# Sums of squares through TensorE: full-precision tiles against one pre-added tile in a high and a low rounded part

## The chip, the core and the metric

The kernel runs on one core of a Trainium2 chip. A core has a matrix engine (TensorE, in the profile PE, its weight loads PEld), a vector engine (VectorE, DVE), a scalar engine (ScalarE, ACT), a general engine (GpSimd, POOL) and a sync engine (SP) that here only issues DMAs. Each engine works through its own list of instructions in order and waits on semaphores for the others. The metric is device time in microseconds (us) from one execution; lower is better.

## The reference

One layer of a diffusion transformer over 512 latent tokens with a prefix of 256 context tokens, in float32, model width 2048. Cut to what matters here:

```python
def _rmsnorm(x, w):
    y = x * rsqrt(mean(x * x, axis=-1) + EPS)
    return y * w

h  = _modulate(_rmsnorm(x,  norm1_w), sh1,  s1)     # 512 latent tokens
hc = _modulate(_rmsnorm(xc, norm1_w), sh1c, s1c)    # 256 context tokens
p = h @ w_in                                        # also hc @ w_in
c_q  = _rmsnorm(p[..., 3072:3456], q_norm_w)        # rank 384, latent tokens only
c_kv = _rmsnorm(p[..., 3456:3712], kv_norm_w)       # rank 256, latent and context
...                                                 # 8 differential heads, 8 latent (MLA) heads
o_da = _rmsnorm(o_da, subln_w) * 0.8                # per head, over its 128 features
x = x + g1 * (concat(o_da, o_mla) @ w_o)
h2 = _modulate(_rmsnorm(x, norm2_w), sh2, s2)       # second norm, over 2048 features
x = x + g2 * _conv_ffn(h2, ...)                     # gated MLP, inner width 5632
return _rmsnorm(x, final_w)
```

Each norm needs, per token, a sum of squares over features.

## The kernel before

Activations lie with features on the 128 partitions and tokens along the free dimension, so a tile is 128 features by 512 latent tokens (`T`), or by 768 tokens (`TT`) with the context. A sum over features is a sum over partitions. The kernel gets it from TensorE: a 128x128 matrix of ones (`ones32`) as weights and a tile of squares as the moving operand give the sum, on every partition, in PSUM; several tiles are summed by accumulating their matmuls. `rstd` (L157) turns the sum into 1/sqrt by Ln and Exp on ScalarE and one Newton step in four VectorE instructions.

The large products split each float32 operand into a high part rounded to the type fp32r and a low part, the rest (`split`, L77: a ScalarE copy and a VectorE subtract), and run three fp32r matmuls, L104 to L106 (`mm3`). The sums of squares instead run their matmul on the float32 tiles themselves; the trace shows each as two MATMUL records. L numbers are lines of the kernel before.

The work runs in stages, by the time in the profiled execution:

- 0 to 180 us: modulation, first norm, the first five feature blocks.
- 180 to 350: `latent_norm` (L428) of the two `ckv` tiles, then ten blocks of input projection (`feature`, L457), each two weight blocks of 1024 columns loaded by `wblock` (L87), then `latent_norm` of the three `cq` tiles, where the value projection starts. Meanwhile VectorE runs the products of the modulation weights with the conditioning vector (`gemv`, L166, recorded at L171).
- 350 to 480: value projection, in two halves. 480 to 700: the eight differential heads.
- 700 to 890: the eight MLA heads. After the scores of head `h` the kernel calls `sub_norm(h)` (L646), which fetches a differential head's output, squares it (L651), sums it (L653), and scales it in place. Between, `weighted_values` (L517) transposes the probabilities (L522), splits them (`wth`, `wtl`, L80 and L81) and multiplies with the values (`po`). For every even head but the last, `latent_pair` (L591) makes the next two heads' queries, keys and values.
- 890 to 1060: output projection. For the first twelve output tiles `add_square` (L699) squares on ScalarE and adds into `ss` on GpSimd (L705). The last four tiles are done by `last_projection` (L998): each is gated on VectorE (L732), stored by a DMA issued from GpSimd (L1022) and squared (L1017), and the second norm's sum is accumulated in PSUM from `ss` (L1036) and the squares of the last four tiles (L1037, L1039, L1042, L1046).
- 1060 to 2440: the gated MLP and the final norm.

Up to about 1010 us a planner orders the instructions of each engine: it walks the program with its own estimates of durations and places what it believes to be ready, so that an edit can also move instructions around it. From the last quarter of the output projection on, the order is written out by hand (`manual_schedule`, for PE, ACT, DVE and SP), in the order of the code. Tiles of a tag share a ring of `bufs` buffers: the tag `nq` in `latent_norm` has one, so that each square waits for the matmul of the one before.

Of the kernel before, what the change touches and what calls it, by code (L numbers as in the profile page):

```python
# [17 lines left out]
P = 128  # L18
D = 2048
KT = D // P  # L20
T = 512
C = 256
TT = T + C
# [29 lines left out]
def layer_kernel(ctx: ExitStack, tc: tile.TileContext, small, rope, c_row, cc_row, x_t, ctx_t, ada, ada_k,  # L53
                 w_g0, w_f, w_v, w_uqn, w_uqr, w_ukv, w_o, w_up0, w_up, w_dn, out_t):
    nc = tc.nc
    pe, ve, sc, gp = nc.tensor, nc.vector, nc.scalar, nc.gpsimd

    cst = ctx.enter_context(tc.tile_pool(name="cst", bufs=1))
# [6 lines left out]
    def nm(s):  # L65
        n[0] += 1
        return f"{s}{n[0]}"
# [55 lines left out]

    ident = cst.tile([P, P], F32, name="ident")
    make_identity(nc, ident)
    ones32 = cst.tile([P, P], F32, name="ones32")
    ve.memset(ones32, 1.0)
    epst = cst.tile([P, 1], F32, name="epst")
    ve.memset(epst, EPS)
# [17 lines left out]
    def apply_rope(out, ps, tmp):  # L147
        t2 = tmp()
        ve.tensor_tensor(out, ps, ropet[:, 0, :], op=ALU.mult)
        ve.stream_shuffle(t2, ps, mask=[i ^ 16 for i in range(32)])  # L150
        ve.tensor_tensor(t2, t2, ropet[:, 1, :], op=ALU.mult)
        ve.tensor_tensor(out, out, t2, op=ALU.add)

    def exp_ln_tables():
        tc.keep_in_program_order(sc.preload_act_table_set("natural_log_exp_and_others"))
# [110 lines left out]
    with tc.manual_schedule(engines={mybir.EngineType.PE, mybir.EngineType.Activation, mybir.EngineType.DVE,  # L266
# [14 lines left out]
        for wide in (cb, ccb):  # L281
            sc.activation(wide[0:1], wide[0:1], AF.Silu)
            s_ = s_tile()
            for j in range(4):
                t = s_[:, j * 512:j * 512 + 512] if j < 2 else b_tile()
# [4 lines left out]
        for kt in range(KT):  # L290
            sq = st.tile([P, TT], F32, tag="h", name=nm("sq"), bufs=3) if kt else sqs
# [52 lines left out]
    for kt in range(KT):  # L344
# [8 lines left out]
        with tc.high_priority():  # L353
            h = st.tile([P, TT], F32, tag="h", name=nm("h"), bufs=3)
            for i, (x, c, m, (hh, hl)) in enumerate(((xs[kt], slice(0, T), modx, hx[kt]),
                                                     (ct, slice(T, TT), modc, hc[kt]))):
                b, t, r = m[:, kt:kt + 1], h[:, c], rinv[:, c]
# [5 lines left out]
        for f in range(5):  # L363
            w = (wh[:, f * P:(f + 1) * P], wl[:, f * P:(f + 1) * P])
# [62 lines left out]

    def latent_norm(tiles, width, dim, wname, dst):  # L428
        s = s_tile()
        cuts = [(0, T)] if width == T else [(0, T), (T, width)]  # L430
        for i, t in enumerate(tiles):
            q = kv.tile([P, TT], F32, tag="nq", name=nm("nq"), bufs=1)
            sc.square(q[:, :width], t)
            for c0, c1 in cuts:
                pe.matmul(s[:, c0:c1], ones32, q[:, c0:c1], start=i == 0, stop=i == len(tiles) - 1)
        r, t1 = (kv.tile([P, TT], F32, tag=g, name=nm(g), bufs=1) for g in ("nr", "n1"))
        t2 = kv.tile([P, TT], F32, tag="nq", name=nm("n2"), bufs=1)
        rstd(r[:, :width], s[:, :width], dim, t1[:, :width], t2[:, :width])
        for i, t in enumerate(tiles):
            ve.scalar_tensor_tensor(out=t, in0=t, scalar=col(wname, i), in1=r[:, :width], op0=ALU.mult, op1=ALU.mult)  # L440
            hl = [kvs.tile([P, TT], F32R, tag=g, name=nm(g))[:, :width] for g in ("kh", "kl")]
            split(hl[0], hl[1], t)
            put(dst[i], hl)
# [9 lines left out]
    q = rtmp()  # L453
# [176 lines left out]
    mb = None  # L630
# [14 lines left out]

    def sub_norm(h):  # L646

        q, rs, t2 = (mb.tile([P, T], F32, tag=g, name=nm(g), bufs=1) for g in ("sq", "sr", "s2"))
        oraw[h] = b2k()
        nc.sync.dma_start(oraw[h], o_d[h])  # L650
        sc.square(q, oraw[h])  # L651
        po = b_tile("f", 2)
        pe.matmul(po, ones32, q, start=True, stop=True)  # L653
        rstd(rs, po, P, mb.tile([P, T], F32, tag="sq", name=nm("s1"), bufs=1), t2)
        ve.scalar_tensor_tensor(out=oraw[h], in0=oraw[h], scalar=subs, in1=rs, op0=ALU.mult, op1=ALU.mult)

# [341 lines left out]
    def last_projection(i):  # L998
        kb, w = jobs[i][1], [h[0] for h in ready[i][:2]]
        if kb < 6:  # L1000
            for j in range(2):
                for d in range(4):
                    project(live["o"], d, kb * 2 + j, w)
            cast(i + 2)
            low(i + 2)
            return
        outs, xr = live["o"], live["xr"]

        def both(d, kbs=(6, 7)):
            for k in kbs:  # L1010
                for kt in (2 * k, 2 * k + 1):
                    project(outs, d, kt, [h[0] for h in ready[i - kb + k][:2]])

        def square(src, c=slice(0, T)):
            if c.start == 0:
                live["q"] = wo.tile([P, T], F32, tag="sq", name=nm("sq"), bufs=2)
            sc.square(live["q"][:, c], src[:, c])  # L1017
            return live["q"]

        def put(d):  # L1020
            gated(12 + d, outs[d], xr[d])
            gp.dma_start(x1_d[12 + d], x1[12 + d])  # L1022
            return square(x1[12 + d])

        if kb == 6:
            both(0)
            both(1)
            cast(i + 2)
            low(i + 2)
            live["q0"] = put(0)  # L1030
            return
        s = s_tile()
        po = s[:, :T]
        both(2)
        q1 = put(1)
        pe.matmul(po, ones32, ss, start=True, stop=False, skip_group_check=True)  # L1036
        pe.matmul(po, ones32, live["q0"], start=False, stop=False, skip_group_check=True)  # L1037
        both(3, (6,))
        pe.matmul(po, ones32, q1, start=False, stop=False, skip_group_check=True)  # L1039
        both(3, (7,))  # L1040
        q2 = put(2)
        pe.matmul(po, ones32, q2, start=False, stop=False, skip_group_check=True)  # L1042
        for c in halves:
            gated(15, outs[3], xr[3], c)
            q3 = square(x1[15], c)
            pe.matmul(po[:, c], ones32, q3[:, c], start=False, stop=True, skip_group_check=True)  # L1046
        gp.dma_start(x1_d[15], x1[15])
        wo.release()
        mem["ff"] = tc.alloc_tile_pool(name="ff", bufs=1, reuse_waits="tile")
        hp = mem["hp"] = tc.alloc_tile_pool(name="hp", bufs=1, side="right", reuse_waits="tile")  # L1050
        r = mem["r"] = hp.tile([P, T], F32, name="nr")
        n1, n2 = (hp.tile([P, T], F32, tag="h", name=nm("n"), bufs=6) for _ in range(2))
        for c in halves:
            sc.activation(r[:, c], po[:, c], AF.Ln, bias=epst, scale=1.0 / D)
            sc.activation(r[:, c], r[:, c], AF.Exp, scale=-0.5)
            ve.tensor_scalar(out=n1[:, c], in0=po[:, c], scalar1=1.0 / D, scalar2=EPS, op0=ALU.mult, op1=ALU.add)
        norm_tiles(0)
        norm_tiles(1)
        for c in halves:
            ve.scalar_tensor_tensor(out=n2[:, c], in0=r[:, c], scalar=-0.5, in1=r[:, c], op0=ALU.mult, op1=ALU.mult)  # L1060
            ve.tensor_tensor(n2[:, c], n2[:, c], n1[:, c], op=ALU.mult)
# [352 lines left out]
```

## Time and profile before

| what | value |
|---|---|
| three runs | 2440.68, 2437.37, 2435.56 us |
| median | 2437.37 us |
| profiled execution, its own time from first to last instruction | 2439.6 us |
| PE busy | 2367.0 us, 97% |
| DVE, ACT, POOL busy | 1735.5 (71%), 1117.0 (46%), 220.2 (9%) us |
| mean granted TensorE clock | 0.992 |

The page gives busy time by engine, the span in 40 slices, the queues, a chain of work that ended last, and groups of instructions. The trace behind it can be asked for windows (busy time of each engine in a stretch) and for a timeline (start, duration, engine, line, operation, output and inputs, and in square brackets the idle time before it and what ended that). Durations of successive matmuls overlap; their pace is the distance between starts.

### The profile page before, as it was taken

What the parts mean: (1) busy time and instruction counts of PE and PEld (TensorE: products, weight loads), DVE (VectorE), ACT (ScalarE), POOL (GpSimd) and SP (SyncE); (2) the same over time, 40 slices, a digit from 0 to 9 for tenths busy, and PEclk for the clock granted to TensorE, in tenths of its full rate; (3) what the DMA queues carried; (4) which work ended last, traced back from release to release, by engine and by line L of the source; (5) the groups of instructions that cost most, each with busy time, mean ns of one, the idle gap of its engine ahead of it and who ended that gap; (6) DMA issues with size and microseconds to landing.
All of it is one profiled execution on the core that took longest, in us unless ns stands there. A gap on an engine that the chain in (4) does not pass through costs nothing.

```text
span 2439.6 us, 32889 instructions
## 1 busy us (share of the span) xinstructions
PE 2367.0 (97%) x12758; PEld 1978.4 (81%) x12758; DVE 1735.5 (71%) x2316; ACT 1117.0 (46%) x1696; POOL 220.2 (9%) x244
## 2 busy tenths in 40 slices
PE   6999999999999999999999999999999999999998
PEld 3678877777777778889888888888888888888888
DVE  6668876388868878378667676767666666666667
ACT  4432121155646542245445454545454545454545
POOL 0000000121100003100111111111111111111110
PEclk9999999999999999999999999999999999999999
DMA  8758889555411149423555555555555565556573
GB/s 300 279 211 309 327 319 330 181 166 144 127 59 44 44 161 349 146 87 113 147 130 143 134 140 137 137 139 136 141 134 143 132 143 132 141 135 140 133 188 111
DMA packets 130707, 403.32 MB, mean 165 GB/s; under 512 B 14323, under 2 KB 25075, under 8 KB 122099
## 3 DMA queue, kind: packets, MB, share of 16 engines
q1 hardware_dynamic: 104118, 350.87, 43.7%
q0 software_dynamic: 25280, 49.30, 11.6%
q8 instruction: 100, 1.64, 0.3%
q10 hardware_dynamic: 1152, 1.05, 0.1%
q14 instruction: 57, 0.47, 0.1%
HBM read 331.68 MB, written 69.48 MB: 164 GB/s over the span
## 4 chain that ended last, share of the span: by engine, by line
PE 76%; DVE 8%; issue 7%; ACT 4%; DMA 3%; POOL 2%; SPq 0%; DVEq 0%; ACTq 0%; POOLq 0%
PE y L1133 11%; PE b L105 9%; PE b L104 9%; PE b L106 9%; PE z L1133 5%; PE y L1135 5%; PE s L104 3%; PE s L105 3%; PE s L106 3%; PE z L1135 3%; PE s L510 3%; PE x L1133 2%; DMA ada<-in_ada 2%; PE b L206 1%; PE f L104 1%
## 5 line engine op out<-in xcount | busy, mean ns | idle before, releaser
L989 DVE TENSOR_TENSOR wl<-wr,wh 128x1024 fp32r<-128x1024 f32 x144 | 176.4, 1225 | 157.8 <-ACT wh L981 157.1
L981 ACT CAST wh<-wr 128x1024 fp32r<-128x1024 f32 x144 | 151.0, 1049 | 234.0 <-PE b L105 118.5
L104 PE MATMUL b<-ah,wh 128*128 128x512 f32 (+1 forms) x664 | 256.8, 387 | 0.0
L105 PE MATMUL b<-al,wh 128*128 128x512 f32 (+1 forms) x664 | 256.7, 387 | 0.0
L106 PE MATMUL b<-ah,wl 128*128 128x512 f32 (+1 forms) x664 | 255.9, 385 | 0.0
L1154 POOL DMA_DIRECT2D x_d<-xs x160 | 139.6, 1004 | 1162.6 <-ACT xs L1153 1159.3
L989 DVE TENSOR_TENSOR wl<-rb,wh 128x1024 fp32r<-128x1024 f32 x123 | 150.0, 1220 | 126.9 <-ACT wh L981 126.8
L981 ACT CAST wh<-rb 128x1024 fp32r<-128x1024 f32 x123 | 129.2, 1050 | 185.7 <-PE b L105 116.1
L989 DVE TENSOR_TENSOR wl<-ws,wh 128x1024 fp32r<-128x1024 f32 x123 | 150.1, 1220 | 90.1 <-ACT wh L981 90.1
L80 ACT CAST wh<-wr 128x1024 fp32r<-128x1024 f32 (+3 forms) x102 | 99.2, 972 | 217.0 <-PE b L106 62.1
L171 DVE CUSTOM_DVE_ANT_0 ada<-ada,cb,smt 128x2048 f32<-128x2048 f32 x64 | 152.5, 2382 | 54.6 <-DMA ada<-in_ada 54.2
L981 ACT CAST wh<-ws 128x1024 fp32r<-128x1024 f32 x123 | 128.2, 1043 | 130.3 <-DVE ws L943 44.3
L1133 PE MATMUL y<-a2k,wh 128*128 128x512 f32 x656 | 164.0, 392 | 0.0
L81 DVE TENSOR_TENSOR wl<-wr,wh 128x1024 fp32r<-128x1024 f32 (+3 forms) x102 | 116.9, 1146 | 62.1 <-ACT wh L80 61.7
L104 PE MATMUL b<-a2k,wh 128*128 128x512 f32 (+1 forms) x376 | 141.6, 377 | 5.9 <-ACT a2k L838 4.3
L106 PEld LDWEIGHTS b<-ah,wl 128*128 128x128 f32 x664 | 124.8, 188 | 25.7
L104 PEld LDWEIGHTS b<-ah,wh 128*128 128x128 f32 x664 | 125.1, 188 | 22.9
L105 PEld LDWEIGHTS b<-al,wh 128*128 128x128 f32 x664 | 125.1, 188 | 21.9
L105 PE MATMUL b<-a2k,wh 128*128 128x512 f32 (+1 forms) x376 | 140.8, 374 | 0.0
L106 PE MATMUL b<-a2k,wl 128*128 128x512 f32 (+1 forms) x376 | 140.0, 372 | 0.0
L1133 PEld LDWEIGHTS y<-a2k,wh 128*128 128x128 f32 x656 | 118.6, 189 | 21.6
L1133 PE MATMUL y<-b2k,wh 128*128 128x512 f32 x410 | 107.8, 393 | 0.0
(454 smaller groups left out, 5757.2 us busy)
## 6 DMA issues: line engine op xcount, KB each, us to landing
ada<-in_ada SPq DMA_DIRECT2D x64, 1024.0 KB, 6.4
rb<-in_w_up SPq DMA_DIRECT2D x123, 512.0 KB, 4.3
wr<-in_w_dn SPq DMA_DIRECT2D x88, 512.0 KB, 4.3
x_d<-xs POOLq DMA_DIRECT2D x160, 256.0 KB, 6.0
wr<-in_w_up SPq DMA_DIRECT2D x53, 512.0 KB, 4.2
wr<-in_w_f SPq DMA_DIRECT2D x34, 512.0 KB, 6.0
ada<-in_ada SPq DMA_DIRECT2D x32, 512.0 KB, 6.4
adak<-in_ada_k SPq DMA_DIRECT2D x32, 512.0 KB, 6.3
```

What stands on the lines that cost most here:

```text
L80: sc.copy(dst_h, src)
L81: ve.tensor_tensor(dst_l, src, dst_h.bitcast(F32), op=ALU.subtract)
L104: pe.matmul(out, st[0], mv[0], start=start, stop=False, **kw)
L105: pe.matmul(out, st[0], mv[1], start=False, stop=False, **kw)
L106: pe.matmul(out, st[1], mv[0], start=False, stop=stop, **kw)
L171: ve.tensor_tensor_reduce(out=junk, in0=w, in1=vec, op0=ALU.mult, op1=ALU.add, scale=1.0, scalar=col("b_ada", j), accum_out=dst[:, j:j + 1])
L510: pe.matmul(s[:, c0:c1], a, b[:, c0:c1], start=i == 0, stop=i == len(mms) - 1)
L981: sc.copy(t, raw[:, k * n_:k * n_ + n_])
L989: ve.tensor_tensor(t, raw[:, k * n_:k * n_ + n_], hi[k].bitcast(F32), op=ALU.subtract)
L1133: pe.matmul(o, w[j][0], hs[j], start=start and j == 0, stop=False, skip_group_check=True)
L1135: pe.matmul(o[:, h0], w[j][1], hs[j][:, h0], start=False, stop=j == 7, skip_group_check=True)
L1154: gp.dma_start(x1_d[dt], x, accum_op=ALU.add)
```

## The change

A new helper, `summed`, takes one tile of squares, copies it to a tile of type fp32r (the high part, ScalarE), subtracts that from the tile on GpSimd (the low part), and runs two fp32r matmuls with the ones instead of the float32 matmul. The matrix of ones is declared fp32r and read as float32 where the old form remains. It is used in three places:

- `latent_norm`: the tiles of squares are added on GpSimd into one tile, which goes through `summed`: one add and one subtract of 128x768 for `ckv`, two adds and one subtract of 128x512 for `cq`.
- `sub_norm`: each head's tile of squares goes through `summed`, eight times.
- `last_projection`: the square of output tile 12 is added into `ss` on GpSimd, and `ss` goes through `summed`, after the first half of the work on the fourth tile. The squares of tiles 13 to 15 stay as they were.

```diff
+    def summed(out, q, hi, lo, start=True, stop=True):
+        w = q.shape[1]
+        hi, lo = hi[:, :w], lo[:, :w]
+        sc.copy(hi, q)
+        gp.tensor_tensor(out=lo, in0=q, in1=hi.bitcast(F32), op=ALU.subtract)
+        for c0, c1 in ((0, T), (T, w)) if w > T else ((0, w),):
+            for i, t in enumerate((hi, lo)):
+                pe.matmul(out[:, c0:c1], onesr, t[:, c0:c1], start=start and i == 0, stop=stop and i == 1,
+                          skip_group_check=True)
...
     def latent_norm(tiles, width, dim, wname, dst):
         s = s_tile()
-        cuts = [(0, T)] if width == T else [(0, T), (T, width)]
+        q = kv.tile([P, TT], F32, tag="nq", name=nm("nq"), bufs=1)
         for i, t in enumerate(tiles):
-            q = kv.tile([P, TT], F32, tag="nq", name=nm("nq"), bufs=1)
-            sc.square(q[:, :width], t)
-            for c0, c1 in cuts:
-                pe.matmul(s[:, c0:c1], ones32, q[:, c0:c1], start=i == 0, stop=i == len(tiles) - 1)
+            if i == 0:
+                sc.square(q[:, :width], t)
+                continue
+            q1 = kv.tile([P, TT], F32, tag="n1", name=nm("n1"), bufs=1)
+            sc.square(q1[:, :width], t)
+            gp.tensor_tensor(out=q[:, :width], in0=q[:, :width], in1=q1[:, :width], op=ALU.add)
+        summed(s, q[:, :width], *(kv.tile([P, TT], F32R, tag=g, name=nm(g), bufs=1) for g in ("nr", "n1")))
...
     def sub_norm(h):
...
-        pe.matmul(po, ones32, q, start=True, stop=True)
+        summed(po, q, *(mb.tile([P, T], F32R, tag=g, name=nm(g), bufs=1) for g in ("sr", "s2")))
...
-            live["q0"] = put(0)
+            gp.tensor_tensor(out=ss, in0=ss, in1=put(0), op=ALU.add)
...
         q1 = put(1)
-        pe.matmul(po, ones32, ss, start=True, stop=False, skip_group_check=True)
-        pe.matmul(po, ones32, live["q0"], start=False, stop=False, skip_group_check=True)
         both(3, (6,))
+        summed(po, ss, *(wo.tile([P, T], F32R, tag="xr", name=nm("xr"), bufs=4) for _ in range(2)), stop=False)
         pe.matmul(po, ones32, q1, start=False, stop=False, skip_group_check=True)
```

More of the change, by code (lines that the diff above doesn't have):

```diff
@@ L125, in layer_kernel @@
     make_identity(nc, ident)
-    ones32 = cst.tile([P, P], F32, name="ones32")
+    onesr = cst.tile([P, P], F32R, name="ones32")
+    ones32 = onesr.bitcast(F32)
     ve.memset(ones32, 1.0)
@@ L646, in sub_norm @@
     def sub_norm(h):
-        q, rs, t2 = (mb.tile([P, T], F32, tag=g, name=nm(g), bufs=1) for g in ("sq", "sr", "s2"))
+        q = mb.tile([P, T], F32, tag="sq", name=nm("sq"), bufs=1)
         oraw[h] = b2k()
@@ L652, in sub_norm @@
         po = b_tile("f", 2)
-        pe.matmul(po, ones32, q, start=True, stop=True)
+        summed(po, q, *(mb.tile([P, T], F32R, tag=g, name=nm(g), bufs=1) for g in ("sr", "s2")))
+        rs, t2 = (mb.tile([P, T], F32, tag=g, name=nm(g), bufs=1) for g in ("sr", "s2"))
         rstd(rs, po, P, mb.tile([P, T], F32, tag="sq", name=nm("s1"), bufs=1), t2)
```

## The prediction

> **What bounds the kernel now.** I read the page's busy line and its chain first, then the windows of the stages that the change touches.
>
> ```profile
> PE 2367.0 (97%) x12758; PEld 1978.4 (81%) x12758; DVE 1735.5 (71%) x2316; ACT 1117.0 (46%) x1696; POOL 220.2 (9%) x244
> PE 76%; DVE 8%; issue 7%; ACT 4%; DMA 3%; POOL 2%; SPq 0%; DVEq 0%; ACTq 0%; POOLq 0%
> ```
>
> ```profile
> 180.00:196.00 16.00, 13.92 (x70) 10.78 (x70) 15.77 (x25) 9.39 (x13) 0.00 (x0) 1.00 0.63 224
> 196.00:250.00 54.00, 54.00 (x310) 47.24 (x309) 45.17 (x61) 11.04 (x15) 0.00 (x0) 1.00 0.89 316
> ...
> 700.00:890.00 190.00, 181.31 (x979) 144.77 (x978) 152.56 (x267) 110.15 (x212) 0.00 (x0) 1.00 0.16 52
> ...
> 734.00:745.00 11.00, 9.88 (x51) 7.14 (x50) 10.89 (x21) 8.16 (x15) 0.00 (x0) 1.00 0.03 5
> 782.00:795.00 13.00, 11.90 (x63) 9.10 (x62) 12.16 (x22) 8.71 (x17) 0.00 (x0) 1.00 0.14 40
> 830.00:842.00 12.00, 10.89 (x56) 7.98 (x55) 11.89 (x23) 8.17 (x15) 0.00 (x0) 1.00 0.09 18
> ```
>
> The columns are window, length, then busy time of PE, PEld, DVE, ACT and POOL. PE is the bound: 97% of the span, and full from 196 to 250, so a microsecond that PE loses just before is never given back. Two stretches are different: from 180 to 196 DVE is busy 15.77 of 16.00, and where the odd MLA heads are normed it is busy 10.89 of 11, 12.16 of 13 and 11.89 of 12. There DVE has nothing to spare either. POOL is empty in all of these.
>
> **What the change removes.** The price of a float32 sum is read in the second norm, by starts on PE:
>
> ```profile
> 1047.36 1.02 PE L1036 MATMUL s<-ss,ones 128*128 128x512 f32 x2
> 1048.22 1.02 PE L1037 MATMUL s<-sq,ones 128*128 128x512 f32 x2
> ...
> 1049.31 0.40 PE L105 MATMUL b<-a2k,wh 128*128 128x512 f32 x1
> 1049.54 0.40 PE L106 MATMUL b<-a2k,wl 128*128 128x512 f32 x1
> ```
>
> From 1047.36 to 1048.22 one float32 sum of 512 columns holds PE 0.86 us; an fp32r matmul holds it 1049.54 - 1049.31 = 0.23, so the pair costs 0.46 and a sum saves 0.40. Half the columns I take at half of that, 0.43 against 2 x 0.12. PE time saved:
>
> - ckv norm: 2 x (0.86 + 0.43) = 2.58 becomes 0.46 + 0.24 = 0.70, saves 1.9.
> - cq norm: 3 x 0.86 becomes 0.46, saves 2.1.
> - head norms: 8 x 0.40 = 3.2.
> - second norm: 2 x 0.86 becomes 0.46, saves 1.3.
>
> Together 8.5 us. DMAs and their queues lose and gain nothing: the stores of L1022 stay where they are in POOL's list, with one add and one subtract between them.
>
> **What it adds.** Every sum now waits for a ScalarE copy and for GpSimd, and PE and ACT take their work in order, so whatever stands behind the low part's matmul, or behind the Ln, waits with it. The prices:
>
> ```profile
> 182.08 0.62 ACT L80 CAST kh<-rt 128x512 fp32r<-128x512 f32 x1 [1.57 <-DVE rt L152]
> 182.61 1.04 ACT L80 CAST wh<-wr 128x1024 fp32r<-128x1024 f32 x1
> ...
> 197.15 0.84 ACT L80 CAST kh<-ckv 128x768 fp32r<-128x768 f32 x1 [0.99 <-DVE ckv L440]
> ```
>
> ```profile
> 919.27 2.62 POOL L705 TENSOR_TENSOR ss<-ss,sq 128x512 f32<-128x512 f32 x1
> ...
> 924.87 2.77 POOL L705 TENSOR_TENSOR ss<-ss,sq 128x512 f32<-128x512 f32 x1
> ...
> 1005.66 1.29 POOL L705 TENSOR_TENSOR ss<-ss,sq 128x512 f32<-128x512 f32 x1
> ```
>
> The copy costs 0.62 at 512 columns and 0.84 at 768. A GpSimd instruction on two 128x512 tiles costs 1.29 to 2.77. For 768 columns no row exists; by columns it is 1.5 x 1.29 = 1.9 alone, at most 1.5 x 2.77 = 4.2; I take 1.9 plus the wait for the DVE instruction in progress. The spread has its cause in DVE's rows:
>
> ```profile
> 918.38 2.35 DVE L171 CUSTOM_DVE_ANT_0 ada<-ada,cb,smt 128x2048 f32<-128x2048 f32 x1
> ...
> 923.11 3.38 DVE L171 CUSTOM_DVE_ANT_0 ada<-ada,cb,smt 128x2048 f32<-128x2048 f32 x1
> ```
>
> The add issued at 919.27 ends about 1.3 after that product does; the product issued at 923.11, while POOL was adding, takes 1.03 longer. They take turns. The Trainium skill, "SBUF — State Buffer", section "SBUF: two separate sides", says so and more sharply: a GpSimd instruction and a DVE instruction with two SBUF inputs hold a shared port exclusively and the loser waits for the whole instruction; the trace agrees (2.62 and 3.38). By that rule alone an add behind a fresh product could take 1.29 + 2.35 = 3.6, an estimate from these rows that no row here reaches; one such case in the cq norm would make the sum below 0.9 longer.
>
> **ckv norm, 179.7 us.** PE's rows before:
>
> ```profile
> 180.57 1.56 PE L435 MATMUL s<-nq,ones 128*128 128x512 f32 x4 [0.51 <-ACT nq L433]
> 183.70 0.50 PE L104 MATMUL b<-a2k,wh 128*128 128x512 f32 x1 [1.57 <-ACT wh L80]
> ...
> 184.72 1.56 PE L435 MATMUL s<-nq,ones 128*128 128x512 f32 x4
> ...
> 186.46 0.40 PE L104 MATMUL b<-a2k,wh 128*128 128x512 f32 x1
> ```
>
> ```profile
> 179.67 0.85 ACT L433 ACTIVATE nq<-ckv 128x768 f32<-128x768 f32 x1
> ```
>
> One sum stood in a gap in which PE waited for weights anyway. In the built order both squares come first (179.67 to 181.3), the GpSimd add waits for DVE's rope instruction to 182.05 and runs to 183.9, the copy comes behind two weight casts, 185.0 to 185.85, the subtract behind one DVE weight subtract, 186.4 to 188.3. On PE only one feature triple, the high part and one context matmul stand ahead of the low part; it starts at 188.4, and with 0.23 + 2 x 0.12 + 0.24 for what stood before 186.46, the next triple starts at 189.1 instead of 186.46: **+2.6**, and PE is full afterwards. Lower end: GpSimd never late, -1.9. Upper end: GpSimd gets in ahead of the rope instruction, whose result gates the first weight cast, another 1.9 to 2: +4.6.
>
> **cq norm, 335.7 us.**
>
> ```profile
> 335.70 1.02 PE L435 MATMUL s<-nq,ones 128*128 128x512 f32 x2
> ...
> 342.70 0.50 PE L104 MATMUL s<-wh,a2k 128*128 128x512 f32 x1 [0.33 <-DVE n L161]
> ```
>
> ```profile
> 336.74 1.23 DVE L81 TENSOR_TENSOR wl<-wr,wh 128x1024 fp32r<-128x1024 f32 x1 [0.22 <-ACT wh L80]
> 339.69 2.35 DVE L171 CUSTOM_DVE_ANT_0 ada<-ada,cb,smt 128x2048 f32<-128x2048 f32 x1 [1.72 <-DMA ada<-in_ada]
> ```
>
> ```profile
> 336.62 0.58 ACT L479 COPY cq<-b 128x512 f32<-128x512 f32 x1
> ```
>
> The last square follows that copy and ends near 337.7; add behind DVE's 336.74 instruction, to 339.2; copy to 339.85; subtract from 339.9. If it goes first it ends at 341.2, if the product of 339.69 does, at 343.3. PE has 15 matmuls (3.4 us) to do, then the high part and one more, and would reach the low part at 339.6. Before, the same work was through at about 342.2, with 0.33 of wait to come. Now it is through at 341.5 or 343.6: **-1.0 to +1.0, taken as 0**, because the product hangs on a transfer's arrival.
>
> **Head norms, 703 to 877.** In heads 0, 2 and 4 a pair's projections stand between the square and the sum (head 0: 703.83 to 733.98): GpSimd is hidden, and 0.40 each is kept. Heads 1, 3, 5, 6 and 7 use the square at once:
>
> ```profile
> 703.83 0.63 ACT L651 ACTIVATE sq<-b2k 128x512 f32<-128x512 f32 x1
> ...
> 733.98 1.02 PE L653 MATMUL f<-sq,ones 128*128 128x512 f32 x2
> ```
>
> Head 1, and then head 6:
>
> ```profile
> 740.62 0.64 ACT L651 ACTIVATE sq<-b2k 128x512 f32<-128x512 f32 x1
> ...
> 742.15 1.02 PE L653 MATMUL f<-sq,ones 128*128 128x512 f32 x2
> 742.24 0.90 ACT L514 ACTIVATE w<-s,m 128x768 f32<-128x768 f32 x1 [0.98 <-DVE m L512]
> ...
> 743.21 0.69 ACT L159 ACTIVATE sr<-f,epst 128x512 f32<-128x512 f32 x1
> ...
> 856.11 0.63 ACT L651 ACTIVATE sq<-b2k 128x512 f32<-128x512 f32 x1
> ...
> 858.47 1.02 PE L653 MATMUL f<-sq,ones 128*128 128x512 f32 x2
> ```
>
> In the built order of these five, between the two matmuls stand at most two others (one or two `po` matmuls, one projection matmul, or one transpose), some 0.1 to 0.46 us of cover, and on ACT, in four of the five, the Ln stands directly behind the copy, with the next `wth` cast behind it. The sum is later by copy + subtract + low part - old sum: 0.62 + 1.29 + 0.23 - 0.86 = 1.3 with GpSimd alone, 2.8 at 2.77. What it costs lies between 0 (PE had other work in progress: the sum started 0.9 us after its square's end in head 1, 1.7 in head 6) and 2.8. I take 1.5, next to the lower row, because DVE's two-SBUF instructions are short here, and because DVE, full in these stretches, stands at its own first step on the sum (L161) with the softmax maxima behind it. 5 x 1.5 - 8 x 0.40 = **+4.3**; ends -3.2 and 5 x 2.8 - 3.2 = +10.8.
>
> **Second norm, 1042 to 1049.**
>
> ```profile
> 1045.68 0.63 ACT L1017 ACTIVATE sq<-b2k 128x512 f32<-128x512 f32 x1 [2.09 <-DVE b2k L732]
> ```
>
> The copy follows this square, 1046.3 to 1046.9; the subtract runs to 1048.3 on a POOL that DVE does not disturb there (L732 reads PSUM). PE, now through with six more matmuls, arrives at 1047.36 + 6 x 0.23 = 1048.7. Covered, so **-1.3**; if the subtract takes 2.77 it ends at 1049.8 and the gain shrinks to -0.2.
>
> **Order elsewhere.** The planner also reorders other work in the MLA heads and the projections. PE idles 190.00 - 181.31 = 8.7 us in the MLA stage; a luckier order could return some, an unluckier one take as much. Taken as 0.
>
> Sum: 2.6 + 0 + 4.3 - 1.3 = **+5.6 us**, or 2445.2 on the profiled execution's span of 2439.6, which lies 2.2 above the median; against the median 2437.4, **2443.0**.
>
> **The rivals.**
>
> - *No wait at all* (the other side): GpSimd is done before PE arrives. All of the 8.5 is kept: 2428.9. For it: the planner put the low parts where it believed them ready, and PE often runs behind. Against it: ckv, where DVE's queue makes GpSimd late by any row. It is decided by one number, the time between high and low part on PE: a subtract shorter than about 0.5 us wins, and the shortest row is 1.29.
> - *Only ckv waits*: in the five heads PE's own lag covers GpSimd. 2.6 - 3.2 - 1.3 = -1.9: 2435.5.
> - *The port decides*: each subtract meets a DVE instruction, 2.77 throughout. 4.6 + 1.0 + 10.8 - 0.2 = +16.2: 2453.6. For it: DVE is full there, and a held DVE instruction delays the maxima too. Against: many DVE instructions of the MLA stage read PSUM. The skill's port rule, named above, would bring this if met every time.
>
> **How the numbers follow.** Forecast 0.48, no wait 0.13, only ckv 0.22, port 0.17. The measurement tells 0.2%, 4.9 us, from no change. The forecast at +5.6 lies just above that: 0.35 of its 0.48 counts as slower, 0.13 as the same. Only-ckv gives 0.18 to the same and 0.04 to faster (a better order); the port all to slower; no wait all to faster. Faster 0.17, same 0.31, slower 0.52. The range leaves out most of the no-wait case and the far half of the port case: 2431 to 2453; the forecast's own is 2439 to 2448.
>
> **What would show it.** In the profile after: PE idle before the low part's matmul, released by POOL, about 2 to 4 us at 186 and 1 to 2 in heads 1, 3, 5, 6, 7; none at 1048; second-norm PE work 1.3 shorter; POOL subtracts at 1.3 with some near 2.5. If the low parts start without idle time before them, the forecast is wrong and the time falls under 2437; if the MLA stage grows by over 8 us with DVE instructions stretched, the port decided.

## The result, and the profile after

The changed kernel takes 2444.61 us (median of 22 runs, 2440.22 to 2452.05), the kernel before 2440.86 us (22 runs, 2435.56 to 2445.87). The ratio is 1.0017, 95% interval 1.0010 to 1.0024: 4 us slower, which is just inside the 0.2% that the prediction called no change. The profiled execution grew from a span of 2439.6 to 2442.8 us, by 3.2.

The page of the changed kernel, its busy line and its chain:

```profile
PE 2362.7 (97%) x12748; PEld 1978.6 (81%) x12748; DVE 1740.9 (71%) x2316; ACT 1121.9 (46%) x1707; POOL 244.9 (10%) x259
PE 84%; DVE 7%; ACT 3%; issue 3%; POOL 1%; DMA 1%; SPq 0%; DVEq 0%; ACTq 0%; POOLq 0%
```

PE is busy 4.3 us less, and the span is longer. So PE waited more, or ran slower for a while; busy time counts a slow matmul as busy. The windows show where. Columns as in the prediction (window, length, busy time of PE, PEld, DVE, ACT, POOL), then the granted TensorE clock, the DMA share and GB/s. First the kernel before, then the changed one:

```profile
180.00:185.00 5.00, 2.92 (x10) 1.56 (x10) 4.89 (x9) 3.43 (x6) 0.00 (x0) 1.00 0.30 121
185.00:193.00 8.00, 8.00 (x43) 6.59 (x43) 7.94 (x13) 3.81 (x5) 0.00 (x0) 1.00 0.72 244
```

```profile
180.00:185.00 5.00, 0.00 (x0) 0.00 (x0) 4.89 (x8) 2.54 (x5) 1.80 (x1) 0.80 0.01 4
185.00:193.00 8.00, 6.11 (x17) 4.48 (x18) 7.36 (x9) 4.12 (x8) 2.43 (x1) 0.50 0.45 161
193.00:200.00 7.00, 7.00 (x40) 6.11 (x40) 6.91 (x11) 2.75 (x5) 0.00 (x0) 0.98 0.94 340
...
700.00:890.00 190.00, 180.70 (x985) 145.13 (x984) 151.01 (x260) 111.70 (x215) 11.85 (x10) 1.00 0.15 47
```

At the `ckv` norm PE now does nothing from 180 to 185, and then issues 17 instructions where it issued 43, at a granted clock of 0.50. In the MLA stage PE's busy time is what it was (180.70 against 181.31).

To follow the cost through the kernel I take the same instruction in both traces: the first copy of a `ckv` tile, the first `cq` copy, the first and last differential head's output copy, the squares of output tile 12 and of the first half of tile 15.

| point | before, us | after, us | shift, us | change of shift, and what lies in between |
|---|---|---|---|---|
| first `ckv` copy | 176.95 | 176.72 | -0.23 | |
| first `cq` copy | 314.13 | 319.68 | +5.55 | +5.8: ckv norm |
| first differential head | 533.88 | 539.90 | +6.02 | +0.5: cq norm and value projection |
| last differential head | 694.94 | 701.25 | +6.31 | +0.3 |
| square of tile 12 | 1042.95 | 1047.33 | +4.38 | -1.9: head norms |
| square of tile 15 | 1053.42 | 1056.57 | +3.15 | -1.2: second norm |
| end of the span | 2439.6 | 2442.8 | +3.2 | 0.0 |

This is one pair of executions. Over all the profiles of this study, the experiments below among them, some of these stretches move by more than the shifts in the table. From the first `cq` copy to the first differential head it takes 219.51 to 224.61 us with the old cq norm and 214.31 to 220.22 with the new one, so the +0.5 is no price of the cq norm. From the last differential head to the square of tile 12 it takes 347.05 to 348.04 us in the four profiles with the old head norms and 346.07 to 347.46 in the nine with the new ones (the eighth experiment aside): by the means the head norms are worth -1.0, not -1.9.

A stricter measure of the ckv norm, which I use for every kernel below, stays on PE: the time from the last matmul ahead of the gap to the 32nd `a2k,wl` matmul behind it (the low part of the weights, one per triple). PE is full again well before that. The rows at its two ends in the kernel before, and the one at its end in the changed kernel:

```profile
179.67 0.39 PE L106 MATMUL b<-a2k,wl 128*128 128x512 f32 x1
...
218.44 0.39 PE L106 MATMUL b<-a2k,wl 128*128 128x512 f32 x1
```

```profile
224.00 0.39 PE L106 MATMUL b<-a2k,wl 128*128 128x512 f32 x1
```

In the changed kernel it starts at 179.44 (row below). That is 218.44 - 179.67 = 38.77 and 224.00 - 179.44 = 44.56 us: **+5.8**. In each profiled kernel that keeps the old ckv norm this stretch lasts 38.74 to 38.77 us, so a few tenths can be read from it.

**The ckv norm.** PE, then VectorE, ScalarE and GpSimd of the changed kernel:

```profile
179.44 0.39 PE L106 MATMUL b<-a2k,wl 128*128 128x512 f32 x1
185.10 0.80 PE L104 MATMUL b<-a2k,wh 128*128 128x512 f32 x1 [5.27 <-ACT wh L80]
185.69 0.63 PE L105 MATMUL b<-a2k,wh 128*128 128x512 f32 x1
186.75 0.80 PE L106 MATMUL b<-a2k,wl 128*128 128x512 f32 x1 [0.43 <-DVE wl L81]
187.35 0.63 PE L163 MATMUL s<-nr,ones 128*128 128x512 f32 x1
...
189.55 0.79 PE L163 MATMUL s<-n,ones 128*128 128x512 f32 x1 [1.36 <-POOL n L160]
...
191.00 0.63 PE L104 MATMUL b<-a2k,wh 128*128 128x512 f32 x1
191.42 0.63 PE L105 MATMUL b<-a2k,wh 128*128 128x512 f32 x1
```

```profile
181.14 2.31 DVE L153 TENSOR_TENSOR rt<-rt,rt 128x512 f32<-128x512 f32 x1
```

```profile
183.48 0.62 ACT L80 CAST kh<-rt 128x512 fp32r<-128x512 f32 x1 [2.46 <-DVE rt L153]
184.01 1.04 ACT L80 CAST wh<-wr 128x1024 fp32r<-128x1024 f32 x1
```

```profile
181.10 1.80 POOL L449 TENSOR_TENSOR nq<-nq,n 128x768 f32<-128x768 f32 x1 [179.38 <-ACT n L448]
187.07 2.43 POOL L160 TENSOR_TENSOR n<-nq,nr 128x768 fp32r<-128x768 f32 x1 [4.17 <-ACT nr L159]
```

Four things add up. The add starts 0.04 us ahead of the last of the VectorE instructions that apply the rotary position embedding (the rope instruction below, L153), which then takes 2.31 us; the same instruction takes 0.68 in the kernel without the add quoted under the eleventh experiment. ScalarE waits for it before it casts the weights. The old sum that ran in PE's gap is gone, so PE is idle 5.27 us in one piece where it was idle 0.51 and 1.57. The low part waits 1.36 for GpSimd. And from 185 to 193 the clock is half: two matmuls start 191.42 - 191.00 = 0.42 apart, against 0.23 before.

**The cq norm.** PE's longest wait there, the window, and GpSimd's two instructions:

```profile
PE s L163 <- ACT nr L159: 2.8, 1, 2.8
```

```profile
345.00:350.00 5.00, 2.26 (x5) 1.35 (x6) 0.79 (x2) 0.83 (x2) 3.18 (x2) 0.69 0.76 294
```

```profile
343.44 2.34 DVE L183 CUSTOM_DVE_ANT_0 ada<-ada,cb,smt 128x2048 f32<-128x2048 f32 x1
```

```profile
343.54 3.36 POOL L449 TENSOR_TENSOR nq<-nq,n 128x512 f32<-128x512 f32 x1 [9.60 <-ACT n L448]
347.63 1.27 POOL L160 TENSOR_TENSOR n<-nq,nr 128x512 fp32r<-128x512 f32 x1 [0.73 <-ACT nr L159]
```

The second add starts 0.10 us behind a fresh modulation product and ends 1.12 us after it: it waited out the whole product. PE idles 2.81 us, at the high part already, and the clock falls again.

**Head 1**, as an example of the five tight ones, on ScalarE, GpSimd and PE, and the groups over all eight heads (first all subtracts by minimum, median and maximum in ns; then PE's waits: total, times, longest):

```profile
749.53 0.62 ACT L159 CAST sr<-sq 128x512 fp32r<-128x512 f32 x1
752.11 0.69 ACT L171 ACTIVATE sr<-f,epst 128x512 f32<-128x512 f32 x1 [1.95 <-PE f L163]
```

```profile
750.23 1.28 POOL L160 TENSOR_TENSOR s<-sq,sr 128x512 fp32r<-128x512 f32 x1 [34.54 <-ACT sr L159]
```

```profile
750.27 0.43 PE L163 MATMUL f<-sr,ones 128*128 128x512 f32 x1
...
751.57 0.50 PE L163 MATMUL f<-s,ones 128*128 128x512 f32 x1 [0.40 <-POOL s L160]
```

```profile
L160 POOL TENSOR_TENSOR s<-sq,sr x8: 1278/1289/1359, 714.3 to 883.4; 128x512 fp32r<-128x512 f32 x8
```

```profile
PE f L163 <- POOL s L160: 1.9, 5, 0.5
```

All eight subtracts run alone, 1.28 to 1.36. Five low parts do wait, 1.9 us in all. ScalarE's Ln comes late (752.11, against 743.21 + 6.3 of shift = 749.5 if nothing had changed), and the stretch as a whole does not grow by it. GpSimd is not the only reason: the square ends at 747.13, but ScalarE's list has a cast and an exponential ahead of the copy, which starts 2.4 us later.

**Second norm**, PE:

```profile
1053.09 0.62 PE L163 MATMUL s<-xr,ones 128*128 128x512 f32 x2
1053.55 1.02 PE L1054 MATMUL s<-sq,ones 128*128 128x512 f32 x2
```

High and low part follow each other without a gap and hold PE 1053.55 - 1053.09 = 0.46 us, where two float32 sums took 2 x 0.86.

### The profile page after: what moved, and what is told of

It is laid out like the page before. It is cut to its first block, busy times and chain, and to the rows that moved or that the text cites. A ratio compares the mean times of both kernels' runs of the same rounds, so it can differ in the third digit from the quotient of the medians.

```text
span 2442.8 us, 32916 instructions
## 1 busy us (share of the span) xinstructions
PE 2362.7 (97%) x12748; PEld 1978.6 (81%) x12748; DVE 1740.9 (71%) x2316; ACT 1121.9 (46%) x1707; POOL 244.9 (10%) x259
## 4 chain that ended last, share of the span: by engine, by line
PE 84%; DVE 7%; ACT 3%; issue 3%; POOL 1%; DMA 1%; SPq 0%; DVEq 0%; ACTq 0%; POOLq 0%
PE y L1148 12%; PE b L105 10%; PE b L104 10%; PE b L106 10%; PE z L1148 6%; PE y L1150 6%; PE s L104 3%; PE s L105 3%; PE s L106 3%; PE z L1150 3%; PE s L525 3%; PE x L1148 2%; PE f L104 1%; PE b L218 1%; PE x L1150 1%
```

## The experiments

Shifts at the ckv norm are differences of the PE stretch defined above against its 38.77 us in the kernel before. "Clock" is the mean granted TensorE clock over all timed runs of a kernel; the kernel before has 0.9914 to 0.9918 in its four sets of runs.

### 1 to 4. One part alone

Each is the kernel before with `summed` and one of its uses.

```diff
 only_ckv:    latent_norm: new form if width == TT, old form otherwise
 only_cq:     latent_norm: new form if width == T, old form otherwise
 only_heads:  sub_norm: new form
 only_norm2:  last_projection: new form
```

> Only the ckv norm in the new form; cq norm, head norms and second norm as before. Theory A, from the two traces (first square of cq's tile copy shifted from 314.13 to 319.68 us): the ckv norm alone costs 5.6 to 6 us, because the GpSimd add gets in ahead of the rope instruction whose result gates the weight casts, TensorE stands over 5 us and then runs slowly for some 8 us. Rival B, as forecast: +2.6, and the rest of the shift is something else in the change. Rival C (a planner's reordering further on is what differs): between -1 and +1 by the first cq copy.

> Only the cq norm in the new form. Theory A, from the two traces (+5.54 at the last cq copy, +5.85 at the first differential score): +0.3 at the end of the value projection, the 2.1 us of saved TensorE time paid back by two waits (2.8 us on the ScalarE copy of the high part, whose add stood behind a VectorE product). Rival B: nothing waits when the ckv norm has not shifted the stage, -1 to -2. Whole kernel: -1 to +1 under A.

> Only the eight head norms in the new form. Theory A, from the two traces (+6.31 before the MLA heads, +4.38 at the square of output tile 12): -2 to -3 us, the saved 8 x 0.40 us less short waits for GpSimd of 0.3 to 1 us in heads 1, 3, 5, 6, 7. Rival B, as forecast: +4.3, the waits cost more than the saving. Rival C: the whole -1.9 was luck of the order in the planner's list, and another list gives anything between -5 and +5; then the sums' own waits do not explain it.

> Only the second norm in the new form, in the part of the code whose order is written by hand, so that nothing else moves. Theory A: -1.2 us, read between the squares of tile 12 and tile 15 (10.47 us before, 9.24 expected), no wait before the low part. Rival B: GpSimd late by up to 1.1 us, the gain shrinks to -0.2.

| kernel | median, us | ratio to before (2441.52) | 95% interval | clock |
|---|---|---|---|---|
| ckv alone | 2447.03 | 1.0027 | 1.0018 to 1.0036 | 0.9895 |
| cq alone | 2439.85 | 0.9993 | 0.9985 to 1.0002 | 0.9916 |
| heads alone | 2438.74 | 0.9997 | 0.9987 to 1.0008 | 0.9919 |
| second norm alone | 2439.51 | 0.9993 | 0.9984 to 1.0002 | 0.9914 |

The ckv norm is the only part that costs: 1.0027 is 6.6 us, and its PE stretch is +6.0. The other three lie a little under the kernel before, and each interval includes 1. The ratios add to +0.27 - 0.07 - 0.03 - 0.07 = +0.10%, against +0.17% measured for all together; the intervals allow both. In the profile of the heads alone the stretch from the last differential head to the square of tile 12 is 1.8 us shorter (1.9 in the changed kernel), and with the second norm alone the stretch between the squares of tiles 12 and 15 is 9.24 us instead of 10.47.

### 5. The change without the ckv part

```diff
 no_ckv, against the changed kernel:
     def latent_norm(...):
+        if width == T:
             (new form)
+        else:
+            (old form: square, float32 matmuls, per tile)
```

> The changed kernel with the ckv norm in its old form; cq norm, head norms and second norm new. Theory A (the ckv norm costs 5.8 us, the rest gains): 5 to 6 us less than the changed kernel and 2 to 4 less than the kernel before, a ratio of 0.9985 to 0.9992. Rival B (the loss is spread over the waits, or comes from what the planner moved): no less than the kernel before.

2438.69 us against 2442.04 before, ratio 0.9991 (0.9982 to 1.0001), PE stretch 38.75, clock 0.9911. Taking the ckv part back returns 0.0026, all that it cost alone.

### 6. Work put into PE's gap

Six dummy float32 sums of the `ckv` tiles into the PSUM tile that the real sum overwrites afterwards; the result is not touched.

```diff
 ckv_clock, against the changed kernel:
             gp.tensor_tensor(out=q[:, :width], in0=q[:, :width], in1=q1[:, :width], op=ALU.add)
+        if width == TT:
+            for t in (tiles[0], tiles[1], tiles[0]):
+                for c0, c1 in ((0, T), (T, TT)):
+                    pe.matmul(s[:, c0:c1], ones32, t[:, c0:c1], start=True, stop=True, skip_group_check=True)
```

> The changed kernel with six more float32 matmuls on the ckv tiles (3.9 us on TensorE) that stand in its gap ahead of the first weights and whose sums are overwritten. They change neither the GpSimd add nor the weights' arrival. Theory A: the gap of 5.3 us is what halves the granted clock from 185 to 193 us; with it filled the clock stays at 1.00 and the kernel is about 2 us faster than the changed kernel, in spite of more work: +3.5 to +4.0 at the first cq copy instead of +5.55. Rival B (the clock has another cause, or the slow pace is hidden behind the wait for GpSimd): no change, or slower by what the extra matmuls take.

2443.85 us, ratio 1.0010 (1.0002 to 1.0019), clock 0.9895, PE stretch +4.9. PE and the clock around the gap:

```profile
183.35 0.49 PE L104 MATMUL b<-a2k,wh 128*128 128x512 f32 x1 [1.40 <-ACT wh L80]
...
185.01 0.79 PE L106 MATMUL b<-a2k,wl 128*128 128x512 f32 x1 [0.60 <-DVE wl L81]
```

```profile
183.00:185.00 2.00, 1.06 (x4) 0.59 (x4) 1.96 (x5) 2.00 (x4) 0.00 (x0) 0.94 0.95 366
185.00:187.00 2.00, 1.99 (x5) 1.70 (x6) 2.00 (x2) 0.24 (x1) 1.68 (x1) 0.50 1.03 269
```

The long gap is gone and the clock holds through it, but it falls to half at 185 all the same, after idle times of 1.40 and 0.60 us. So the experiment did not give the clean case it was made for. The traces show what happened: the clock changes only on a grid of 3.41 us (last section), and 1.76 us of these two idle times lie in one step of it, from 181.36 to 184.77. The kernel before is idle for 1.86 us of its step from 180.12 to 183.53 and keeps the clock. Between 1.38 and 1.86 us of idle time the traces hold both outcomes; what decides there stays open.

### 7. The add and the subtract on VectorE

```diff
 ckv_vector, against the changed kernel:
     def latent_norm(...):
+        eng = ve if width == TT else gp
...
-            gp.tensor_tensor(out=q[:, :width], in0=q[:, :width], in1=q1[:, :width], op=ALU.add)
+            eng.tensor_tensor(out=q[:, :width], in0=q[:, :width], in1=q1[:, :width], op=ALU.add)
```

(and the same engine for the subtract in `summed`)

> The changed kernel with the add and the subtract of the ckv norm on VectorE instead of GpSimd, all else the same. Theory A: what costs is that GpSimd's add holds up the rope instruction (2.31 us instead of 0.68) and with it the weight casts; on VectorE the add takes 0.95 us in line, the gap on TensorE falls from 5.3 to 3 to 4.5 us, and the ckv norm costs 2 to 4 us instead of 5.8. Rival B (the chain of square, add, copy, subtract is too long on any engine, VectorE being full): as slow as the changed kernel.

2443.73 us, ratio 1.0013 (1.0002 to 1.0023), clock 0.9894. The first `cq` copy is 5.1 us late against the kernel's own start, but half of that is ScalarE's order at the copy (it stands behind a weight cast that waits 4.32 us for a transfer); on PE the stretch is +2.5. PE's first matmul:

```profile
181.77 0.80 PE L104 MATMUL b<-a2k,wh 128*128 128x512 f32 x1 [3.64 <-ACT wh L80]
```

No GpSimd instruction runs here, the weights come as early as before (4.03 us after the last matmul, in both), no low part waits, and still PE is idle 3.64 us in one piece, and the 0.80 for a first matmul shows the slow clock. So GpSimd in the gap is not all of it. By time this kernel is not told apart from the changed one (1.0013 against 1.0017). The profiled execution is the shortest of its twelve runs (clock 0.992, against 0.9894 on average), so its +2.5 may not stand for the others.

### 8. Each head's subtract done twice

```diff
 heads_double, against the changed kernel, in sub_norm alone:
         gp.tensor_tensor(out=lo, in0=q, in1=hi.bitcast(F32), op=ALU.subtract)
+        gp.tensor_tensor(out=lo, in0=q, in1=hi.bitcast(F32), op=ALU.subtract)
```

The same values are written twice.

> The changed kernel with the GpSimd subtract of each head norm done twice, so that each sum comes 1.3 us later. Theory A (in the five tight heads TensorE waits only for what its own lag does not cover, 0.4 us each): between +2 and +6 over the changed kernel, 0.4 to 1.2 us per tight head. Rival B (ScalarE and VectorE take the delay up): less than +1. Rival C, as the forecast priced a late sum: 5 x 1.3 = +6.5 or more.

2454.24 us, ratio 1.0060 (1.0047 to 1.0073): 0.0043 over the changed kernel, 10 us. PE's waits for the low part (total, times):

```profile
  PE f L165: 7.2, 5
```

They grow from 1.9 to 7.2 us, so of each added 1.3 us subtract (7.2 - 1.9) / 5 = 1.06 reaches PE: the cover of the first subtract is used up. The time grows by about 10 us, twice what these waits hold. That is above theory A's range (+2 to +6) and by its size rival C's (+6.5 or more), the price that the forecast put on a late sum. In the traces the growth lies between the last differential head and the square of tile 12, 355.28 us against 346.07. The planner's order of the MLA heads changed as well, and the rest was not separated.

### 9. The ckv norm without its add

```diff
 ckv_noadd, against the changed kernel:
-            gp.tensor_tensor(out=q[:, :width], in0=q[:, :width], in1=q1[:, :width], op=ALU.add)
+            if width == T:
+                gp.tensor_tensor(out=q[:, :width], in0=q[:, :width], in1=q1[:, :width], op=ALU.add)
```

> The changed kernel, with the GpSimd add of the ckv norm left out (the second tile is squared, but the sum holds the first tile's squares alone, so the ckv norm is computed wrongly); copy, subtract and both matmuls stay. Theory A, the add gets in ahead of the rope instruction, holds it, starves PE of weights for 5.27 us and so halves the clock: the wait for the first weight cast returns to 1.5 to 2 us, the rope instruction to about 0.7, the granted clock in 180 to 193 us stays at 1.00, and the first cq copy comes +0 to +2 us against before, counted from the kernel's own first ckv copy, instead of +5.8; time about 4 us under the changed kernel, ratio 0.9995 to 1.0005. Rival B, the chain of copy, subtract and low part is the cost on any engine: the first cq copy stays at +4 to +6 and the ratio at 1.0012 to 1.002.

The sum then holds the first tile's squares alone. 2445.71 us, ratio 1.0017 (1.0008 to 1.0026), clock 0.9888, PE stretch +5.1:

```profile
182.01 0.79 PE L104 MATMUL b<-a2k,wh 128*128 128x512 f32 x1 [3.64 <-ACT wh L80]
...
186.46 0.79 PE L163 MATMUL s<-n,ones 128*128 128x512 f32 x1 [1.37 <-POOL n L160]
```

```profile
185.00:193.00 8.00, 6.63 (x24) 5.67 (x24) 7.36 (x11) 3.08 (x4) 1.41 (x1) 0.55 0.43 151
```

Theory A, which I held at this point, falls: the rope instruction is back at 0.68 us and the first weights come as early as before (4.03 us after the last matmul), and the cost is nearly all there. The wait did not return to 1.5 to 2 us but to 3.64, because what had split it, the old sum of the first tile, is not there: 0.51 + 1.57 of idle time and the 1.56 of that sum are 3.64. And after 3.64 us of idle time the clock is half, from 181.9 to 192.2.

### 10. The ckv norm without its low part

```diff
 ckv_nolow, against the changed kernel, for ckv alone:
-        gp.tensor_tensor(out=lo, in0=q, in1=hi.bitcast(F32), op=ALU.subtract)
...
-            for i, t in enumerate((hi, lo)):
+            for i, t in enumerate((hi,)):
```

> The changed kernel, with the subtract and the low part's matmuls of the ckv norm left out (the ckv sum is rounded, so less exact); the add, the copy and the high part stay. Theory A: the rope instruction still waits for the add, PE for weights 4 to 5 us, the clock still drops in 180 to 193 us, and the first cq copy stays at +3.5 to +5 against before, counted from the kernel's own first ckv copy; ratio about 1.001. Rival B, the low part is what costs: +0 to +2 and a ratio of 0.9993 to 1.0003.

2440.86 us, ratio 1.0002 (0.9993 to 1.0010), clock 0.9902, PE stretch +2.9 (+4.3 by the `cq` copy, which again stands behind a weight cast):

```profile
183.53 0.80 PE L104 MATMUL b<-a2k,wh 128*128 128x512 f32 x1 [5.27 <-ACT wh L80]
```

The wait of 5.27 and the slow clock are as theory A expected, the time is rival B's. Both had part of it: without the low part's wait PE is continuously busy from 185.2, the clock is full again from 188.3, and the slow episode ends 10.4 us after the last matmul ahead of the gap instead of 13.8. A late low part costs twice, by its wait and by holding the clock down.

### 11. Heads and second norm alone

```diff
 heads_norm2: the kernel before, with the new sub_norm and last_projection
```

> The kernel before, with the change made in the head norms and the second norm alone. If the parts add: -1.8 us in the heads and -1.2 in the second norm, 3 us under before, ratio 0.9984 to 0.9992. If the planner's other orders take it back, as the single parts cannot tell: 0.9993 to 1.0005. The second norm's stretch from the square of tile 12 to the first half square of tile 15 is 9.2 us against 10.5 in either case.

2436.96 us against 2440.49, ratio 0.9988 (0.9979 to 0.9997), clock 0.9916. The parts add, and this kernel has the lowest ratio of the study; the intervals of the fifth and the twelfth overlap with its own. The rope instruction of the ckv norm, here without an add beside it:

```profile
179.30 0.68 DVE L153 TENSOR_TENSOR rt<-rt,rt 128x512 f32<-128x512 f32 x1
```

### 12. The first tile left in the gap

The first tile's squares go through the old float32 matmuls, the second tile's through copy, subtract and two matmuls; there is no add.

```diff
 ckv_split, against the changed kernel:
                 sc.square(q[:, :width], t)
+                if width == TT:
+                    for c0, c1 in ((0, T), (T, TT)):
+                        pe.matmul(s[:, c0:c1], ones32, q[:, c0:c1], start=True, stop=False, skip_group_check=True)
+                    q = kv.tile([P, TT], F32, tag="nq", name=nm("nq"), bufs=1)
+                    sc.square(q, tiles[1])
+                    break
                 continue
```

> The changed kernel, but in the ckv norm the first tile's squares go through the old float32 matmuls (which stood in PE's gap before) and only the second tile's through copy, subtract and two matmuls; no add. Theory D, the old first sum split PE's gap into 0.51 and 1.57 us, and taking it out made one gap of 3.6 us (5.3 with the add) that halves the clock: the two waits return to about 0.5 and 1.6 us, the granted clock in 180 to 193 us is 0.95 to 1.00, and the first cq copy comes at -1 to +2 us against before, counted from the kernel's own first ckv copy (5.8 in the changed kernel, 5.1 without the add); ratio 0.9992 to 1.0006. Rival B, copy, subtract and low part cost it with any first half: the low part is late, the clock falls all the same, the first cq copy stays at +3.5 to +6 and the ratio at 1.001 to 1.002.

2439.45 us against 2441.46, ratio 0.9991 (0.9982 to 1.0000), clock 0.9913, PE stretch +1.6:

```profile
180.87 1.56 PE L448 MATMUL s<-nq,ones 128*128 128x512 f32 x4 [0.51 <-ACT nq L445]
184.00 0.50 PE L104 MATMUL b<-a2k,wh 128*128 128x512 f32 x1 [1.57 <-ACT wh L80]
...
185.65 0.49 PE L106 MATMUL b<-a2k,wl 128*128 128x512 f32 x1 [0.59 <-DVE wl L81]
...
189.06 0.50 PE L163 MATMUL s<-n,ones 128*128 128x512 f32 x1 [1.28 <-POOL n L160]
```

```profile
185.00:193.00 8.00, 6.13 (x33) 4.99 (x33) 8.00 (x11) 4.84 (x6) 2.30 (x1) 1.00 0.56 198
```

Theory D holds. The gap is split as before, the clock stays at 1.00, and although the low part still waits 1.28 and the weights 0.59, the norm costs 1.6 us instead of 5.8. The ninth experiment is the closest comparison: it has no add either and the same copy, subtract and low part, and without the first tile's old sum in the gap it costs 5.1. By the `cq` copy the shift is 2.4, a little over the expected 2; the copy stands behind a weight cast here too. The profiled execution is also 5.0 us shorter than the kernel before from the first `cq` copy to the first differential head (214.73 against 219.75), which I do not ascribe to the edit, because this stretch moves by as much from kernel to kernel.

## Why the prediction was right, and where it was not

The sum came out near: +5.6 forecast on the profiled span, +3.2 there and +4 by the timed ratio. Its sign and the range hold, and the forecast's own range too (2439 to 2448, with 2437.4 x 1.0017 = 2441.5). But two terms were wrong, one by +3.2 and one by -6.2 in this pair of traces, in opposite directions. That the total came out near is luck.

| term | forecast | measured in the pair of traces |
|---|---|---|
| ckv norm | +2.6 (-1.9 to +4.6) | +5.8 |
| cq norm | 0 (-1.0 to +1.0) | +0.5, with the value projection |
| head norms | +4.3 (-3.2 to +10.8) | -1.9 (-1.0 by the means above) |
| second norm | -1.3 | -1.2 |

- **ckv norm, mis-sized, beyond its upper end.** The step that failed is "One sum stood in a gap in which PE waited for weights anyway". I counted that sum as free and its removal as neutral. It was what cut the gap into 0.51 and 1.57 us; without it, the clock is half from the next matmul on. The rows give the sum. The add holds the rope instruction and so the first weights, 5.66 us after the last matmul instead of 4.03: +1.6, which I had, but only as the upper end. Waits of 0.43 and 1.36: +1.8. Less PE work, one float32 sum of 1.29 outside the gap against 0.70: -0.6. The clock: 185.10 to 193.3 less those waits is 6.4 us of matmuls at 0.42 where 0.23 was due, 6.4 x (1 - 0.23 / 0.42) = +2.9. Together +5.7, against 5.8. The same sum without the add is 1.8 - 0.6, and for the clock (182.01 to 192.2 less 1.8) x 0.45 = 3.8, +5.0 against 5.1; with the first tile left in the gap it is 0.59 + 1.28 - 0.6 = +1.3 against 1.6. So the forecast's mechanism, a late low part, is real and measured by the twelfth experiment at 1.6; the clock, absent from the prediction, is the largest single term. The profile of before held the warning: I read its granted clock of 1.00 at this place as a given and not as something the old order kept up.
- **cq norm, right in kind.** The product went first, as the prediction left open ("because the product hangs on a transfer's arrival"). The add took 3.36, between the 2.77 seen before and the 3.6 that I estimated from the Trainium skill's port rule ("SBUF — State Buffer", section "SBUF: two separate sides"); the trace agrees with that rule here. PE waited 2.81 us and the clock fell to 0.69, which would be more than +1.0; but a later wait of the value projection became shorter, from 2.1 to 0.7 us in the rows below, and with it a slow stretch went that the kernel before has behind that wait (clock 0.50 from 415.6 to 419.1). Together they gave most of it back in this pair of traces. Alone, this part is 0.07% faster, and its interval includes no change.

```profile
PE s L104 <- DVE kl L81: 2.1, 1, 2.1
```

```profile
PE s L104 <- DVE kl L81: 0.7, 1, 0.7
```

- **Head norms, the wrong sign.** "I take 1.5" per tight head was almost four times too much. The delay of the sum was no smaller than computed (Ln 2.6 late in head 1), but PE waited only 1.9 / 5 = 0.4 per head for the low part, since it had other work until then. 1.9 - 8 x 0.40 = -1.3, between the -1.9 of this pair and the -1.0 of the means; that the late Ln cost nothing is read from this agreement and not shown by itself. By time the heads alone are not told apart from the kernel before, but their interval ends at +0.08%, 2 us, and the forecast's +4.3 lies outside it. The rival "only ckv waits" had this part nearly right. Doubling the subtract shows how near the edge it was: nearly all of the second 1.3 reaches PE, and the kernel loses 2 us per tight head.
- **Second norm, right**: covered, and at the forecast size.
- **The port** decides nothing in the heads, where each of the eight subtracts ran alone. It does act in both latent norms: rope instruction 2.31 for 0.68, subtract 2.43 at 187.07, add 3.36.
- **What would show it**: PE idle 1.36 before the low part at the ckv norm, where 2 to 4 was said, and 5.27 more where nothing was said; 0.5 at most in the heads, where 1 to 2 was said; none in the second norm, as said. By the prediction's own test, low parts without idle time before them, the heads came close to contradicting it; the total hid that.

## What to carry to other kernels

A matmul that runs inside a gap of PE is not free to remove: before taking it out, add up the idle time that then falls within 3.4 us, and look at the granted clock of the windows behind it, since a gap of 3.6 us here halved the clock for 6.8 us in one kernel and 10.2 in another. Where a sum has to wait for a second engine, keep the pieces that are ready early on the old path and send only the last through the longer chain. And a total that comes out right is no evidence for its terms: shifts read at fixed instructions in both traces show the errors at once, as long as they are larger than what the same stretch moves by between kernels that share the code.

## What the runs showed of the hardware

- After 5.27 and after 3.64 us without a matmul the granted clock was 0.50. This is what the Trainium skill says in "TensorE: Matmul & The Clock Gate", section "Part 1: The HAM clock gate (the "warmup" mystery)": half clock after an idle window of about 3.4 us, full clock after a busy one; the trace agrees with its number. But the clock also fell after shorter idle times: 2.81 us at the cq norm, and 1.40 with 0.60 in the sixth experiment, while 0.51, 1.57, 0.59 and 1.28 within 9 us in the twelfth did not lower it. The same section calls the window free-running, and the traces agree: in each of the 14 the clock changes only on a fixed grid of 3.41 us, which no gap restarts, and each of the 92 slow stretches (the one that a kernel's end cuts off left out) lasts 3.4, 6.8 or 10.2 us. In the changed kernel they run from 183.0 to 193.3 at the ckv norm and from 346.9 to 353.7 at the cq norm, and their beginnings are 48 steps apart.
- The traces tie the clock to PE's idle time within one step, counted by its matmul records. Of the steps at full clock, all 81 with 1.87 us or more of idle time were followed by a slow step, 17 of the 55 with 1.38 to 1.86, and none with less. The clock came back only behind a step with at most 0.41 us of idle time; so a low part that comes late within a slow step prolongs the slow stretch, to 10.2 us in the changed kernel against 6.8 without the low part.
- The slow episode is there in the timed runs too, not only in the profiled one. The mean granted clock over the runs is 0.9884 to 0.9895 in each kernel whose ckv norm has the low part and not the first tile's float32 sum, 0.9902 without the low part, and 0.9911 to 0.9919 where that sum stays in the gap. A difference of 0.9916 - 0.9890 = 0.0026 of 2440 us is 6.3 us at full clock, or 12.7 us at half.
- A GpSimd instruction that starts 0.04 us ahead of a VectorE instruction with two SBUF inputs stretched it from 0.68 to 2.31 us, although GpSimd itself was busy only 1.80.
